# Hybrid decoder block on one core: top-k 2 of the gathered token tile moved into the first steps of the dense expert stage, one-hots and fill products shared out by thirds, 19 + 3 u-tiles ahead

## The chip, the cores and the metric

The kernel runs on one core of a Trainium2 chip. The metric is the device time of one execution in microseconds (us), lower is better. A profile of one execution goes with it: the span of that execution, the busy time of each engine (PE is TensorE's matmuls, PEld its weight loads, DVE is VectorE, ACT is ScalarE, POOL is GpSimd, SP is SyncE, which issues most transfers), the waits, and the order of the instructions in time.

## The reference

512 tokens of width 1024 go through attention and a linear recurrence side by side, then through an expert layer and a gated embedding. The change is in the expert layer, which for each token scores 2 x 128 keys per head, takes the best 16 of each half, then the best 16 of their sums, and mixes the 128 experts so chosen out of 16384:

```
    v1, i1 = lax.top_k(s1, PEER_TOPK)
    v2, i2 = lax.top_k(s2, PEER_TOPK)
    cand = (v1[..., :, None] + v2[..., None, :]).reshape(B, S, PEER_HEADS, PEER_TOPK * PEER_TOPK)
    ...
    top_s, pos = lax.top_k(cand, PEER_TOPK)
    idx = jnp.take_along_axis(cand_idx, pos, axis=-1)
    g = jax.nn.softmax(top_s, axis=-1).astype(x.dtype)
    ...
        act = jax.nn.gelu(jnp.einsum('chkd,cd->chk', ue, xt))
        return jnp.einsum('chk,chkd->cd', gt * act, ve)
```

"Top-k 1" is the choice of 16 keys in each half, "top-k 2" the choice of 16 sums, with the softmax and the expert numbers.

## The kernel before, in words

The 512 tokens are four tiles of 128. **One tile is gathered** (tile 0, NTG = 1): for each of its 128 chosen experts the rows of u and v are fetched by an indirect transfer (line 938, issued by POOL) and used on DVE (lines 946 and 953). **Three tiles are dense**: all 16384 experts are multiplied on PE, and a weight table that is zero but for the chosen experts picks out what counts. There are 128 expert groups e of 128 experts. A *u-tile* of group e is gelu(u_e x), a 128 x 384 tile; it times the weights gives `hf`, which times v_e is added to `y`.

Every operand in fp32 is split into a high and a low part (`split`, lines 54 on ACT and 55 on DVE or POOL) and multiplied three times (`mm3`, lines 64 to 66). Some u-tiles are made as plain fp32 products instead, without a split (`fill`, line 743); these are the *fill products*, 8 for each u-tile, and they are put between other work on PE.

**The weight stage** (some 573 to 785 us of the span) runs 96 groups n, 32 for each dense tile; a third of the stage is one tile. Group n makes the weights of four tokens from a one-hot `bm` (line 863, DVE) and a weighted one-hot `am`. Which engine makes `am` is written in the string PAT: D is DVE (four instructions, line 857), P is POOL (four, line 857), A is ACT (eight, lines 853 and 854). `w_make` multiplies them on PE (line 870), copies the result on ACT to `wst` (line 875), and every eight groups SP writes 2 MB to `wdram`. The steps of top-k 2 are functions in a list, taken from it while n runs: those of tile 2 in the first third (with what is left of top-k 1), those of tile 3 in the second, those of the gathered tile 0 in the last. A third takes its steps in its first 23 groups, and the tile of the next third can start only when they are done. A list has 13 steps: one that builds the candidates, four that find the maxima of two heads each, the start of the softmax, one that splits the positions, four `pick` that look the numbers up, the end of the softmax, and the expert numbers. After group n, `fill` makes fill products up to a due number.

**The dense stage** (from 785 us) runs the groups e = 0 to 127 under a manual schedule: each engine takes its instructions in the order of the program text. Step e loads and splits v_(e+1) (`v_split`, `h_make`), loads and splits u_(e+AHEAD+1), multiplies u-tile e+AHEAD (from e = EXTRA on), fetches gathered rows up to `rate(e)`, uses those fetched one step earlier, and ends with the 18 products of v_e (`v_mm`). Before the loop stand N4 fill tiles and three u-tiles made with splits. The buffers of v and h are double, so PE needs in step e what DVE has made during step e-1. When the u-tiles are done, `pw_load` brings the eight parts of the last gate's matrix, one every second step, and v's low part is made on POOL in every second step. The queue of SP takes its transfers in program order too.

Of the kernel before, what the change touches and what calls it, by code (L numbers as in the profile page):

```python
# [18 lines left out]
NT = S // 128  # L19
KD = D // 128  # L20
EPS = 1e-6
NEG = -1e30
NTG = 1
NTD = NT - NTG
TD = NTD * 128
PAT = "DPADPPADPPADPDAP"
EXTRA = 4
AHEAD = 21
N4, F0 = 22, 5
NCAND = 80  # L30
# [6 lines left out]
def trunk_kernel(ctx: ExitStack, tc: tile.TileContext, x, xT, pT, small, sinkb, rows, w_in, w_ua, w_ul,  # L37
                 w_ab, w_o, w_q, k12, uT, vP, uN, w_pg, w_pp, out):
    nc = tc.nc
# [545 lines left out]
    def u_gelu(e, ps):  # L585
# [5 lines left out]
        acts[e] = a  # L591

    with tc.tile_pool(name="topk", bufs=1, side="right") as T:
        vals = T.tile([128, NT, 16, 16], F32, name="vals")
        idxu = T.tile([128, NT, 16, 16], U32, name="idxu")
        x2f = T.tile([128, KD, TD], F32, name="x2f")
# [3 lines left out]
        def small(name, dt=F32):  # L600
            return T.tile([128, 128], dt, name=name, tag=name, bufs=1)

        def topk2(t, cuts=((0, 8),)):
# [5 lines left out]
            def begin(lo, hi):  # L609
                def run():  # L610
                    if lo == 0:
                        L["idf"] = T.tile([128, 16, 16], BF16, name="idf", tag="idf", bufs=1)
                        L["ii"] = L["idf"].rearrange("p (h z) k -> p h z k", z=2)
                        L["cand"] = T.tile([128, 8, NCAND], F32, name="cand", tag="cand", bufs=1)
                        L["cand2"] = T.tile([128, 8, NCAND], F32, name="cand2", tag="cand2", bufs=1)
                        top[t] = T.tile([128, 8, 16], F32, name="top", tag="top", bufs=1)
                        posu[t] = T.tile([128, 8, 16], U32, name="posu", tag="posu", bufs=1)
                    hs, n = slice(lo, hi), hi - lo
                    nc.vector.tensor_copy(L["idf"][:, 2 * lo:2 * hi], idxu[:, t, 2 * lo:2 * hi])
                    vv = vals[:, t].rearrange("p (h z) k -> p h z k", z=2)  # L620
# [21 lines left out]
            def soft0():  # L642
                g = gg if t < NTG else T.tile([128, 128], F32, name="g", tag="g", bufs=2)
# [26 lines left out]
            def soft1():  # L670
                g = gs[t]
                g3 = g.rearrange("p (h k) -> p h k", h=8)
                sg = T.tile([128, 8], F32, name="sgs", tag="sgs", bufs=2)
                nc.vector.tensor_reduce(sg, g3, AX.X, OP.add)
                nc.vector.reciprocal(sg, sg)
                nc.vector.tensor_tensor(g3, g3, sg[:, :, None].to_broadcast([128, 8, 16]), OP.mult)

            def pick(z, part):
                def run():
                    if part == 0:  # L680
                        L["i", z] = T.tile([128, 128], F32, name=f"i{z}", tag=f"i{z}", bufs=1)
                    hs = slice(4 * part, 4 * part + 4)

                    eq = T.tile([128, 4, 16, 16], BF16, name="eq", tag="eq", bufs=1)
                    ab3 = L["ab"][z].rearrange("p (h k) -> p h k", h=8)[:, hs]
                    nc.vector.tensor_tensor(eq, iota[:, None, None, 0:16].to_broadcast([128, 4, 16, 16]),
                                            ab3[:, :, :, None].to_broadcast([128, 4, 16, 16]), OP.is_equal)
                    nc.vector.tensor_tensor(eq, eq, L["ii"][:, hs, z, None, :].to_broadcast([128, 4, 16, 16]), OP.mult)
                    nc.vector.tensor_reduce(L["i", z].rearrange("p (h k) -> p h k", h=8)[:, hs], eq, AX.X, OP.add)
                return run  # L690

            def end():
                i0, i1 = L["i", 0], L["i", 1]
                if t < NTG:
                    f = T.tile([128, 128], F32, name="fi", tag="fi", bufs=1)
                    nc.vector.scalar_tensor_tensor(f, i0, 128.0, i1, op0=OP.mult, op1=OP.add)
# [57 lines left out]
        with tc.manual_schedule():  # L754
# [33 lines left out]
            def topk1(hh, t):  # L788
                def run():
                    s = scs[hh][:, t * 128:(t + 1) * 128]  # L790
                    v, ix = vals[:, t, hh, :], idxu[:, t, hh, :]
                    w = T.tile([128, 128], F32, name="mr", tag="mr", bufs=3)
# [53 lines left out]
        def a_make(n):  # L846
            t, q = NTG + n // 32, n % 32
            kind = PAT[n % len(PAT)]
            tr, trn = trs[t], trns[t]
# [32 lines left out]
        with tc.manual_schedule():  # L882
            for _ in range(NWR):
                f_load()
            for k, step in enumerate(first):
                fill((F0 * KD * (k + 1)) // len(first))
                step()
            later = [topk2(NTG + 1), topk2(NTG + 2), [s_ for t in range(NTG) for s_ in topk2(t)]]
            later[0] = [f_ for _, f_ in rest] + later[0]
# [4 lines left out]
            def start(n, limit):  # L894
                for m in range(n, min(n + 7, NGRP)):
                    if m // 32 <= limit and m not in begun and m - n <= lead[PAT[m % len(PAT)]]:
                        begun.add(m)
                        a_make(m)
            nb = 0
            for n in range(NGRP):  # L900
# [167 lines left out]
    with tc.manual_schedule():  # L1068
# [17 lines left out]
        for e in range(128):  # L1086
# [96 lines left out]
```

## Time and profile before

| what | us |
|---|---|
| device time, median of 3 runs | 1842.68 (1839.93 to 1848.08) |
| device time of the profiled execution | 1839.95 |
| its span | 1838.2 |
| PE busy in the span | 1735.0 (94%) |
| DVE busy | 1349.1 (73%) |
| ACT busy | 775.7 (42%) |
| POOL busy | 593.0 (32%) |

The spans are counted from the first to the last instruction, so 1.75 us of the execution lie around them. Matmuls overlap each other, so the duration of one is longer than the distance to the next: the time of a row of matmuls is read from the starts, not from the durations. "Idle before" of an instruction is how long its engine stood still ahead of it, and "<-" names what ended that.

### The profile page before, as it was taken

How to read it: one execution, taken by the hardware profiler on the slowest of the kernel's cores; microseconds unless marked ns; L12 is line 12 of the kernel's file. 1: busy time of each engine (PE TensorE's matmuls, PEld its weight loads, DVE VectorE, ACT ScalarE, POOL GpSimd, SP SyncE). 2: the span in 40 equal slices, each digit the busy share in tenths (PEclk: the TensorE clock that was granted, in tenths of full speed). 3: DMA queues.
4: the chain of work that ended last, by engine and by line, in shares of the span. 5: the costliest groups of instructions: out<-in, count | busy, mean ns of one | idle time of the engine just before them, and what ended most of it. 6: DMA issues, size and time to landing. Idle time of an engine off the chain costs nothing.

```text
span 1838.2 us, 23709 instructions
## 1 busy us (share of the span) xinstructions
PE 1735.0 (94%) x8503; PEld 1476.1 (80%) x8503; DVE 1349.1 (73%) x2636; ACT 775.7 (42%) x1253; POOL 593.0 (32%) x465
## 2 busy tenths in 40 slices
PE   6998899999989699989999999999999999999997
PEld 4877777778866477779999999999999998998775
DVE  6545675556998988947877878788887877865766
ACT  3446657333324577733333333333333333333432
POOL 0000000012315689923433434344434443411210
PEclk9999999999999999999999999999999999999999
DMA  5222225452222244388897988989989889863711
GB/s 190 103 92 87 92 88 170 142 187 97 77 69 103 92 184 184 151 305 311 310 350 286 330 321 293 336 291 330 328 284 337 302 299 339 296 257 134 288 48 69
DMA packets 150311, 392.86 MB, mean 214 GB/s; under 512 B 11824, under 2 KB 62256, under 8 KB 148528
## 3 DMA queue, kind: packets, MB, share of 16 engines
q1 hardware_dynamic: 108720, 245.92, 36.9%
q0 software_dynamic: 37440, 136.33, 21.0%
q10 hardware_dynamic: 4032, 9.08, 1.3%
q8 instruction: 67, 1.10, 0.2%
q14 instruction: 52, 0.43, 0.1%
HBM read 355.64 MB, written 35.65 MB: 213 GB/s over the span
## 4 chain that ended last, share of the span: by engine, by line
PE 72%; DVE 19%; ACT 4%; DMA 2%; issue 2%; ACTq 0%; DVEq 0%; SPq 0%
PE y L64 9%; PE y L65 9%; PE y L66 9%; PE u L66 8%; PE u L64 8%; PE u L65 8%; PE bpj L66 3%; PE bpj L64 3%; PE bpj L65 3%; PE u L743 3%; DVE bm L863 2%; PE bg L870 1%; DVE am L857 1%; DVE idxu L797 1%; DVE idxu L794 1%
## 5 line engine op out<-in xcount | busy, mean ns | idle before, releaser
L64 PE MATMUL y<-vh,hxh 128*128 128x512 f32 x768 | 302.1, 393 | 13.0 <-ACT hxh L54 13.0
L65 PE MATMUL y<-vl,hxh 128*128 128x512 f32 x768 | 301.5, 393 | 0.0
L66 PE MATMUL y<-vh,hxl 128*128 128x512 f32 x768 | 301.4, 392 | 0.0
L66 PE MATMUL u<-x2h,wl 128*128 128x384 f32 x848 | 285.2, 336 | 2.0 <-DVE wl L55 2.0
L64 PE MATMUL u<-x2h,wh 128*128 128x384 f32 x848 | 285.2, 336 | 0.8 <-ACT wh L54 0.8
L54 ACT ACTIVATE vh<-vr 128x1024 fp32r<-128x1024 f32 x128 | 135.8, 1061 | 354.8 <-issue 329.0
L65 PE MATMUL u<-x2l,wh 128*128 128x384 f32 x848 | 284.0, 335 | 0.0
L55 DVE TENSOR_TENSOR wl<-wr,wh 128x1024 fp32r<-128x1024 f32 x154 | 188.4, 1225 | 102.6 <-ACT wh L54 101.9
L938 POOL DMA_INDIRECT gb<-in_vP_dram,vg x128 | 175.7, 1373 | 232.2 <-DVE yg L953 204.0
L938 POOL DMA_INDIRECT gb<-in_uN_dram,ug x128 | 166.8, 1303 | 252.5 <-DVE scr L946 228.8
L857 POOL TENSOR_SCALAR am<-iota,tr 128x128 f32<-128x128 f32 x168 | 179.4, 1081 | 70.4 <-ACT tr L706 45.6
L55 POOL TENSOR_TENSOR wl<-wr,wh 128x1024 fp32r<-128x1024 f32 x18 | 43.2, 2404 | 483.0 <-ACT wh L54 477.4
L54 ACT ACTIVATE wh<-wr 128x1024 fp32r<-128x1024 f32 x172 | 180.1, 1048 | 35.8 <-PE bpj L65 21.0
L55 DVE TENSOR_TENSOR vl<-vr,vh 128x1024 fp32r<-128x1024 f32 x118 | 144.4, 1224 | 65.2 <-ACT vh L54 63.1
L54 ACT ACTIVATE hxh<-hf 128x384 fp32r<-128x384 f32 x128 | 67.2, 525 | 267.8 <-DVE hf L975 267.8
L64 PEld LDWEIGHTS y<-vh,hxh 128*128 128x128 f32 x768 | 145.0, 189 | 42.6 <-ACT hxh L54 15.4
L953 DVE SCALAR_TENSOR_TENSOR yg<-gb,cg,yg 128x1024 f32<-128x1024 f32 x127 | 162.9, 1282 | 20.3 <-DMA gb<-in_vP_dram,vg 17.9
L66 PEld LDWEIGHTS y<-vh,hxl 128*128 128x128 f32 x768 | 145.0, 189 | 32.7 <-DVE hxl L55 1.5
L946 DVE SCALAR_TENSOR_TENSOR scr<-gb,x2t 128x1024 f32<-128x1024 f32 x128 | 156.5, 1223 | 16.1 <-DMA gb<-in_uN_dram,ug 13.9
L65 PEld LDWEIGHTS y<-vl,hxh 128*128 128x128 f32 x768 | 145.2, 189 | 26.2
L64 PEld LDWEIGHTS u<-x2h,wh 128*128 128x128 f32 x848 | 159.2, 188 | 5.8 <-ACT wh L54 1.9
L65 PEld LDWEIGHTS u<-x2l,wh 128*128 128x128 f32 x848 | 159.6, 188 | 4.4
(322 smaller groups left out, 3218.4 us busy)
## 6 DMA issues: line engine op xcount, KB each, us to landing
vr<-in_vP_dram SPq DMA_DIRECT2D x128, 512.0 KB, 9.0
wr<-in_uT_dram SPq DMA_DIRECT2D x120, 512.0 KB, 9.1
wt<-wdram SPq DMA_DIRECT2D x32, 768.0 KB, 8.2
wdram<-wst SPq DMA_DIRECT2D x11, 2048.0 KB, 7.2
wr<-in_w_in_dram SPq DMA_DIRECT2D x38, 512.0 KB, 3.3
wr<-in_w_q_dram SPq DMA_DIRECT2D x16, 512.0 KB, 3.3
gdram<-gf ACTq DMA_DIRECT2D x16, 256.0 KB, 2.2
wr<-in_w_ul_dram SPq DMA_DIRECT2D x8, 512.0 KB, 3.3
```

The lines of the kernel that those rows point to most:

```text
L54: nc.scalar.activation(hi, src, AF.Copy)
L55: (lo_eng or nc.gpsimd).tensor_tensor(lo, src, hi.bitcast(F32), OP.subtract)
L64: nc.tensor.matmul(ps, lh, rh, start=first, stop=False)
L65: nc.tensor.matmul(ps, lh, rl, start=False, stop=False)
L66: nc.tensor.matmul(ps, ll, rh, start=False, stop=last)
L743: nc.tensor.matmul(fps[0], raws[e][:, k * 128:(k + 1) * 128], x2f[:, k, :], start=k == 0, stop=k == KD - 1)
L794: nc.vector.max_index(ix[:, 0:8], v[:, 0:8], s)
L857: (nc.vector if kind == "D" else nc.gpsimd).tensor_scalar(am[:, j, :], iota, tr[:, 0, c:c + 1], tr[:, 2, c:c + 1], op0=OP.is_equal, op1=OP ...
L863: nc.vector.tensor_tensor(bm, iota[:, None, :].to_broadcast([128, 4, 128]), trs[t][:, 1, 4 * q:4 * q + 4, None].to_broadcast([128, 4, 128] ...
L938: nc.gpsimd.indirect_dma_start(out=b, out_offset=None, in_=src, in_offset=bass.IndirectOffsetOnAxis(ap=idx[:, k:k + 1], axis=0))
L946: nc.vector.scalar_tensor_tensor(scr, b, 1.0, x2t, op0=OP.mult, op1=OP.mult, accum_out=dots[:, k:k + 1])
L953: nc.vector.scalar_tensor_tensor(yg, b, cg[:, k:k + 1], yg, op0=OP.mult, op1=OP.add)
```

## The change

The dense stage takes over the top-k 2 of the gathered tile: its 13 steps go into steps e = 0 to 4, three a step, behind the splits that the step makes for e+1. For this the tiles that top-k 2 works on move to a pool that stays open (`TK`), and the staging tile of the last gate's matrix has one buffer instead of two. The gathers start later (`rate` is 2.7 a step from e = 5 on; before 1.3 a step from e = 0, then 2.6) and end at the same step, 99 or 100. The tiny copy that held the gathers back until the first weights had landed (`gate`) goes. Three u-tiles fewer are made as fill products (19 instead of 22) and three more in the dense loop, which makes them up to e = 108 instead of 106. The engine of each one-hot is now written down for each third: in the first two thirds one DVE group in 16 becomes an ACT group (4 D, 7 P, 5 A), in the last two POOL groups in 16 become DVE groups (7 D, 5 P, 4 A; before 5 D, 7 P, 4 A). The fill products are 44 in each of the first two thirds and 24 in the last, where there were 1.51 a group throughout.

```
-PAT = "DPADPPADPPADPDAP"
-EXTRA = 4
-AHEAD = 21
-N4, F0 = 22, 5
+PATS = "DPAPDPAPPADPAPDA", "DPAPDPAPPADPAPDA", "DPADPADPDPADPADD"
+EXTRA = 3
+AHEAD = 19
+N4, F0 = 19, 5
...
+    TK = ctx.enter_context(tc.tile_pool(name="lists", bufs=1, side="right"))
...
-            kind = PAT[n % len(PAT)]
+            kind = PATS[n // 32][n % 16]
...
-            later = [topk2(NTG + 1), topk2(NTG + 2), [s_ for t in range(NTG) for s_ in topk2(t)]]
+            later = [topk2(NTG + 1), topk2(NTG + 2), []]
...
-                fill(F0 * KD + (n + 1) * (NF - F0) * KD // (NGRP - 6))
+                m = n + 1
+                fill(F0 * KD + 44 * min(m, 64) // 32 + (24 * max(0, m - 64)) // 26)
...
-        raw = PW.tile([128, 1024], F32, name="wgr", tag="wgr", bufs=2)
+        raw = PW.tile([128, 1024], F32, name="wgr", tag="wgr", bufs=1)
...
-        return min(256, int(2.6 * (e + 1) - 1.4 * max(0, e + AHEAD - 127) - 1.3 * min(EXTRA, e + 1)))
+        return min(256, max(0, int(2.7 * (e - 4))))
...
-
-        gate = E.tile([128, 1], F32, name="gate")
-        nc.gpsimd.tensor_copy(gate, wts[0][:, 0, 0, 0:1])
+        gathered = [s_ for t in range(NTG) for s_ in topk2(t)]
...
+            for step in gathered[3 * e:3 * e + 3]:
+                step()
             for j in range(g0, rate(e)):
                 g_fetch(j)
```

DVE at the border from the second to the last third, before: behind one-hots of the second third come the candidates (`idf`, `cand`) and the first maxima (`top`, `posu`) of the gathered tile's list, mixed with one-hots.

```order
L863 TENSOR_TENSOR bm<-iota,tr 128x512 x3
L619 CAST idf<-idxu 128x256
L622 TENSOR_TENSOR cand<-vals 128x8x16
L624 TENSOR_TENSOR cand<-vals 128x8x56
L627 TENSOR_TENSOR cand<-vals 128x8x8
L857 TENSOR_SCALAR am<-iota,tr 128x128 x4
L863 TENSOR_TENSOR bm<-iota,tr 128x512
L635 MAX top<-cand 128x8
```

The same border in the changed kernel, where the one-hots' lines are 867 and 861: behind the softmax of tile 3 (`sgs`, `g`) there are one-hots alone, up to the end of the stage.

```order
L678 TENSOR_REDUCE sgs<-g 128x8
L679 RECIPROCAL sgs<-sgs 128x8
L680 TENSOR_TENSOR g<-g,sgs 128x128
L867 TENSOR_TENSOR bm<-iota,tr 128x512 x3
L861 TENSOR_SCALAR am<-iota,tr 128x128 x4
L867 TENSOR_TENSOR bm<-iota,tr 128x512 x4
```

The whole list of the gathered tile has left the last third.

DVE in step e = 3 of the dense loop, before: the parts for v_4 and h_4, the low part of u-tile 25, and one use of a gathered row (`scr`).

```order
L55 TENSOR_TENSOR vl<-vr,vh 128x1024
L975 TENSOR_TENSOR hf<-act,wt 128x384
L55 TENSOR_TENSOR hxl<-hf,hxh 128x384
L55 TENSOR_TENSOR wl<-wr,wh 128x1024
L946 SCALAR_TENSOR_TENSOR scr,dots<-gb,x2t 128x1024
```

The same step in the changed kernel:

```order
L55 TENSOR_TENSOR vl<-vr,vh 128x1024
L980 TENSOR_TENSOR hf<-act,wt 128x384
L55 TENSOR_TENSOR hxl<-hf,hxh 128x384
L55 TENSOR_TENSOR wl<-wr,wh 128x1024
L690 TENSOR_TENSOR eq<-iota,aa 128x1024
L692 TENSOR_TENSOR eq<-eq,idf 128x1024
L693 TENSOR_REDUCE i_6830<-eq 128x64
L690 TENSOR_TENSOR eq<-iota,bb 128x1024
L692 TENSOR_TENSOR eq<-eq,idf 128x1024
L693 TENSOR_REDUCE i_6835<-eq 128x64
L678 TENSOR_REDUCE sgs<-gg 128x8
L679 RECIPROCAL sgs<-sgs 128x8
```

Three steps of top-k 2 stand there now ahead of the next step's `vl`, in the place of the use of the gathered row.

ACT in steps e = 1 and 2 of the dense loop of the changed kernel; before, `vh` and `hxh` alternate there with nothing between them.

```order
L54 ACTIVATE hxh<-hf 128x384
L651 ACT_TABLE_LOAD
L651 ACTIVATE gg<-gg 128x128
L54 ACTIVATE vh<-vr 128x1024
L54 ACTIVATE hxh<-hf 128x384
L54 ACTIVATE wh<-wr 128x1024
```

The exponential of the gathered tile's softmax, which needs DVE's four maxima steps, now stands ahead of the high part of v_3.

## Rows read from the trace of the kernel before

**Rows 1.** Busy time of each engine in three stretches, with granted clock and DMA.
```profile
core 0: us, PE busy (x) PEld busy (x) DVE busy (x) ACT busy (x) POOL busy (x), PEclk, DMA share, GB/s
656.00:720.00 64.00, 60.81 (x359) 47.08 (x358) 57.40 (x166) 48.71 (x107) 60.38 (x56) 1.00 0.48 181
...
802.00:850.00 48.00, 46.88 (x216) 40.66 (x217) 34.60 (x48) 17.38 (x24) 14.40 (x10) 0.96 0.85 304
850.00:1000.00 150.00, 150.00 (x761) 136.85 (x760) 118.55 (x167) 52.94 (x74) 61.30 (x48) 1.00 0.88 323
```

**Rows 2.** Chain that ended last, last third: start us, us, what, count.
```profile
720.50 0.66 issue
...
722.41 1.03 DVE am L857 x4
...
767.28 0.65 PE u L743 x2
767.93 0.89 PE bg L870 x8
...
785.29 1.53 DMA wdram<-wst
```

**Rows 3.** Groups of instructions on ACT, 720 to 782 us: busy, mean ns, idle.
```profile
L875 ACT ACTIVATE wst<-bg 128x512 f32<-128x512 f32 x31 | 17.7, 590 | 11.8 <-PE bg L870 11.7
L854 ACT ACTIVATE am<-am,tr,trn 128x128 f32<-128x128 f32 x32 | 15.8, 493 | 1.1
L853 ACT ACTIVATE am<-iota,trn 128x128 f32<-128x128 f32 x32 | 12.4, 388 | 0.0
```

**Rows 4.** DVE in order of time, one maxima step: start us, us, instruction.
```profile
660.27 0.23 DVE L635 MAX8 top<-cand 128x8 f32<-128x80 f32 x1
...
662.91 1.37 DVE L863 TENSOR_TENSOR bm<-iota,tr 128x512 f32<-128x512 f32 x2
```

**Rows 5.** DVE in order of time, positions step and first pick of the gathered tile.
```profile
744.02 0.31 DVE L658 TENSOR_SCALAR q8u<-posu 128x128 uint32<-128x128 uint32 x1
...
746.94 1.22 DVE L686 TENSOR_TENSOR eq<-iota,aa 128x1024 bf16<-128x1024 f32 x1
...
750.05 0.68 DVE L863 TENSOR_TENSOR bm<-iota,tr 128x512 f32<-128x512 f32 x1
```

**Rows 6.** DVE in order of time, start of the dense stage.
```profile
799.76 1.23 DVE L55 TENSOR_TENSOR vl<-vr,vh 128x1024 fp32r<-128x1024 f32 x1 [8.71 <-ACT vh L54]
...
803.37 1.23 DVE L55 TENSOR_TENSOR vl<-vr,vh 128x1024 fp32r<-128x1024 f32 x1 [0.77 <-ACT vh L54]
804.51 0.55 DVE L975 TENSOR_TENSOR hf<-act,wt 128x384 f32<-128x384 f32 x1
805.65 0.56 DVE L55 TENSOR_TENSOR hxl<-hf,hxh 128x384 fp32r<-128x384 f32 x1 [0.59 <-ACT hxh L54]
...
821.04 1.22 DVE L55 TENSOR_TENSOR wl<-wr,wh 128x1024 fp32r<-128x1024 f32 x1 [0.39 <-ACT wh L54]
```

**Rows 7.** PE in order of time, first dense steps: first products of v and u tiles.
```profile
802.06 0.80 PE L64 MATMUL y<-vh,hxh 128*128 128x512 f32 x1 [5.43 <-ACT hxh L54]
...
821.06 0.44 PE L64 MATMUL u<-x2h,wh 128*128 128x384 f32 x1 [0.42 <-ACT wh L54]
...
826.27 0.39 PE L64 MATMUL y<-vh,hxh 128*128 128x512 f32 x1
...
830.38 0.34 PE L64 MATMUL u<-x2h,wh 128*128 128x384 f32 x1
...
838.68 0.34 PE L64 MATMUL u<-x2h,wh 128*128 128x384 f32 x1
```

**Rows 8.** The page's costliest groups: splits of v on ACT, uses of gathered rows.
```profile
L54 ACT ACTIVATE vh<-vr 128x1024 fp32r<-128x1024 f32 x128 | 135.8, 1061 | 354.8 <-issue 329.0
...
L953 DVE SCALAR_TENSOR_TENSOR yg<-gb,cg,yg 128x1024 f32<-128x1024 f32 x127 | 162.9, 1282 | 20.3 <-DMA gb<-in_vP_dram,vg 17.9
```

**Rows 9.** Transfers issued, by tile: count, KB each, median us to landing.
```profile
wgr<-in_w_pg_dram SPq DMA_DIRECT2D x8, 512.0 KB, 6.1
```

More of the change, by code (lines that the diff above doesn't have):

```diff
@@ L591, in u_gelu @@
         acts[e] = a
+    TK = ctx.enter_context(tc.tile_pool(name="lists", bufs=1, side="right"))
     with tc.tile_pool(name="topk", bufs=1, side="right") as T:
-        vals = T.tile([128, NT, 16, 16], F32, name="vals")
-        idxu = T.tile([128, NT, 16, 16], U32, name="idxu")
+        vals, idxu = [], []
+        for t in range(NT):
+            P = TK if t < NTG else T
+            vals.append(P.tile([128, 16, 16], F32, name=f"vals{t}"))
+            idxu.append(P.tile([128, 16, 16], U32, name=f"idxu{t}"))
         x2f = T.tile([128, KD, TD], F32, name="x2f")
@@ L600, in small @@
         def small(name, dt=F32):
-            return T.tile([128, 128], dt, name=name, tag=name, bufs=1)
+            return TK.tile([128, 128], dt, name=name, tag=name, bufs=1)
         def topk2(t, cuts=((0, 8),)):
@@ L611, in run @@
                     if lo == 0:
-                        L["idf"] = T.tile([128, 16, 16], BF16, name="idf", tag="idf", bufs=1)
+                        L["idf"] = TK.tile([128, 16, 16], BF16, name="idf", tag="idf", bufs=1)
                         L["ii"] = L["idf"].rearrange("p (h z) k -> p h z k", z=2)
[L614 to L617, printed above, removed]
+                        L["cand"] = TK.tile([128, 8, NCAND], F32, name="cand", tag="cand", bufs=1)
+                        L["cand2"] = TK.tile([128, 8, NCAND], F32, name="cand2", tag="cand2", bufs=1)
+                        top[t] = TK.tile([128, 8, 16], F32, name="top", tag="top", bufs=1)
+                        posu[t] = TK.tile([128, 8, 16], U32, name="posu", tag="posu", bufs=1)
                     hs, n = slice(lo, hi), hi - lo
-                    nc.vector.tensor_copy(L["idf"][:, 2 * lo:2 * hi], idxu[:, t, 2 * lo:2 * hi])
-                    vv = vals[:, t].rearrange("p (h z) k -> p h z k", z=2)
+                    nc.vector.tensor_copy(L["idf"][:, 2 * lo:2 * hi], idxu[t][:, 2 * lo:2 * hi])
+                    vv = vals[t].rearrange("p (h z) k -> p h z k", z=2)
                     cand = L["cand"]
@@ L642, in soft0 @@
             def soft0():
-                g = gg if t < NTG else T.tile([128, 128], F32, name="g", tag="g", bufs=2)
+                g = gg if t < NTG else TK.tile([128, 128], F32, name="g", tag="g", bufs=2)
                 gs[t] = g
@@ L672, in soft1 @@
                 g3 = g.rearrange("p (h k) -> p h k", h=8)
-                sg = T.tile([128, 8], F32, name="sgs", tag="sgs", bufs=2)
+                sg = TK.tile([128, 8], F32, name="sgs", tag="sgs", bufs=2)
                 nc.vector.tensor_reduce(sg, g3, AX.X, OP.add)
@@ L680, in run @@
                     if part == 0:
-                        L["i", z] = T.tile([128, 128], F32, name=f"i{z}", tag=f"i{z}", bufs=1)
+                        L["i", z] = TK.tile([128, 128], F32, name=f"i{z}", tag=f"i{z}", bufs=1)
                     hs = slice(4 * part, 4 * part + 4)
-                    eq = T.tile([128, 4, 16, 16], BF16, name="eq", tag="eq", bufs=1)
+                    eq = TK.tile([128, 4, 16, 16], BF16, name="eq", tag="eq", bufs=1)
                     ab3 = L["ab"][z].rearrange("p (h k) -> p h k", h=8)[:, hs]
@@ L694, in end @@
                 if t < NTG:
-                    f = T.tile([128, 128], F32, name="fi", tag="fi", bufs=1)
+                    f = TK.tile([128, 128], F32, name="fi", tag="fi", bufs=1)
                     nc.vector.scalar_tensor_tensor(f, i0, 128.0, i1, op0=OP.mult, op1=OP.add)
@@ L790, in run @@
                     s = scs[hh][:, t * 128:(t + 1) * 128]
-                    v, ix = vals[:, t, hh, :], idxu[:, t, hh, :]
+                    v, ix = vals[t][:, hh, :], idxu[t][:, hh, :]
                     w = T.tile([128, 128], F32, name="mr", tag="mr", bufs=3)
@@ L895, in start @@
                 for m in range(n, min(n + 7, NGRP)):
-                    if m // 32 <= limit and m not in begun and m - n <= lead[PAT[m % len(PAT)]]:
+                    if m // 32 <= limit and m not in begun and m - n <= lead[PATS[m // 32][m % 16]]:
                         begun.add(m)
```

## The prediction

> **What bounds the kernel now.** I read the stretches of the span first, then the chain of waits, then the two stretches that the change touches, instruction by instruction. In the dense stage PE sets the time: it is busy 150.00 of 150 us while DVE has 118.55 [rows 1]. A step there takes 8.30 us, from 830.38 to 838.68, of which the 18 products of v take 4.11 (826.27 to 830.38) and a u-tile the other 4.19 [rows 7]. So what is added to PE there is paid in full, and what is added to DVE is hidden while PE has a step in hand. The weight stage is different: in its second third DVE (57.40), POOL (60.38) and PE (60.81) all lie near the 64 us [rows 1]. The chain of the last third starts on DVE at 720.50, goes over to PE before 767.28 and ends with the last `wst` at 785.29, 64.8 us in all [rows 2].
>
> **The weight stage, per part.** A maxima step of top-k 2 takes 662.91 - 660.27 = 2.65 us [rows 4], a pick 750.05 - 746.94 = 3.11, the positions step 746.94 - 744.02 less one `bm` of 0.68 = 2.24 [rows 5]. The other twelve small instructions I put at the 0.22 that one of the ten in the positions step takes: 2.7. The list is 4 x 2.65 + 4 x 3.11 + 2.24 + 2.7 = 28.0 us of DVE, which leave the last third.
>
> What is left there: DVE 32 x 0.68 for `bm` [rows 5] and 14 groups of 1.03 [rows 2], 36 us. PE 32 groups of 0.89 and 24 fill products of 0.65 [rows 2] (767.28 shows one, in two passes), 44 us. ACT 32 copies of 0.59 and eight groups of four pairs of 0.49 + 0.39 [rows 3], 47 us if nothing overlaps. POOL ten groups at 60.38/56 = 1.08 an instruction [rows 1], 43 us. So DVE is out of the way, and what is late next is ACT, with PE and POOL close behind. The third cannot fall below 47; in-order queues waiting for each other I price at 5.5, between nothing and the 11 that would leave it at 58. I take 52.5, **-12.3 us** (-18 to -7).
>
> In each of the first two thirds DVE loses two groups of 1.03; ACT gains two of 3.5, and has room, as it is busy 48.71 of 64 [rows 1]. Some ten groups at a third's end, where PE leads, carry 0.13 fill products fewer, 10 x 0.13 x 0.65 = 0.9. Against more stands POOL: it keeps its 56 instructions, 60.38 of 64 us. I take 2.5 a third, **-5.0** together (0 to -8). The sum for the stage is -17.3.
>
> **Three u-tiles from fill to the dense loop.** Their fill products are in the sum above. On PE, which sets the dense stage, they cost 3 x 4.19 = **+12.6 us**; two stand at e = 107 and 108, one at e = 3.
>
> **The list in the first dense steps.** Here DVE is behind PE. I count from T = 799.76, when DVE starts on v_0, and walk both engines. One step's parts for v and h take 2.76 on DVE (803.37 to 805.65, and 0.48 until the next can start), the low part of a u-tile 0.39 + 1.14 [rows 6]. Without the change PE runs from T + 2.3 and ends step 6 at T + 47.2 (838.68 and one step of 8.30) [rows 7]. With it:
> - e = 0: h_1 done at 6.4 [rows 6], then the candidates and two maxima steps, until 12.6.
> - e = 1: v_2 and h_2 until 15.4, two maxima steps and the softmax's start until 20.9.
> - e = 2: ACT's exponential, which I put at 0.3 by the 0.39 of an instruction of its size [rows 3], stands ahead of the high part of v_3, 1.06 [rows 8]; DVE starts at 22.3, ends v_3, h_3 at 25.0 and the low part of u-tile 22 at 26.6, then positions and two picks until 35.0.
> - e = 3: v_4, h_4 until 37.8, u-tile 23 until 39.3, two picks and the softmax's end until 46.2.
> - e = 4: v_5, h_5 until 49.0, u-tile 24 until 50.5, the expert numbers until 51.4. From e = 5 on DVE has slack again.
>
> PE: v_0 and v_1 end at 12.5 (the first four v tiles of before took 2.2 more than 4 x 4.11, from 802.06 to 821.06 less a wait of 0.42 [rows 7]). v_2 must wait until 15.0. A u-tile that meets its low part as it is made ends 826.27 - 821.04 = 5.2 after DVE starts on that part [rows 6, 7]: u-tile 22 ends at 30.6, v_3 at 34.7; u-tile 23 at 43.4, v_4 at 47.5; u-tile 24 at 54.6, v_5 at 58.7; u-tile 25 and v_6 follow without a wait, until 67.0. That is 19.8 later than before, 4.2 of which is the u-tile at e = 3, already counted. The rest, **+15.6 us**, is a wait of PE for DVE that was not there (14 to 19).
>
> PE's gaps in this walk are 2.5, 6.3, 3.5 and 1.9 us. After its gap of 5.43 at 802.06 the first product took 0.80 where a later one takes 0.39, and the granted clock of that stretch is 0.96, that is partly at 1.2 instead of 2.4 GHz [rows 1, 7]; v_0 lost the 2 us above. I leave the clock out of the sum, since after the larger gaps PE waits for DVE again, which covers a slower tile. The Trainium skill, "TensorE: Matmul & The Clock Gate", section "Why this matters for your kernels", warns against idle gaps between bursts of matmuls, because the clock drops back to half. [...]
>
> **What I cost at nothing.** The gathers start later and end at the same step; their 2.7 uses a step lie beside PE, and the cover is thin (a rival below). `pw_load` with one buffer can ask for its next part only when DVE has finished the last one, two steps earlier. Of two steps of 4.11 its own two splits, 1.06 and 1.23 like those of v [rows 6, 8], leave 5.9 us; the transfer lands in 6.1 at the median [rows 9], now with more transfers queued ahead of it than it will have. So nothing, or at most some 2 us for each of seven. Removing `gate` frees a wait of POOL that nothing hangs on any more.
>
> **Sum.** -17.3 + 12.6 + 15.6 = +10.9. The profiled execution took 1839.95, so 1851; it lies 2.7 below the median of its three runs, 1842.68, and on that scale the forecast is **1854 us**, slower by 0.6%. A measurement of this kernel can tell 0.5% from no change, 9.2 us.
>
> **Rivals.**
> 1. *The thirds give more than I take* (the other side). If the last third falls to ACT's 47 and the first two to POOL's 60.4 and the like, the stage saves 18 + 8 = 26; with the wait at 14 the sum is +1, 1843, no change. For it speaks that all four engines are near balance by count; against it, that POOL is full in two thirds and that ACT's queue holds `wst` behind eight one-hot instructions. It decides from a saving of some 20 us on. It would take 29 to win.
> 2. *The gathers pace DVE.* A step with three uses is 2.76 + 1.53 + 3 x (1.28 + 0.16 of waiting, 20.3/127) [rows 8] = 8.6 us of DVE, one with two 7.2. At 2.7 uses the mean is 8.2, just under PE's 8.30. If the waits for rows double with the denser fetches (the transfer engines are 0.88 busy [rows 1]), it is 8.6, and 0.3 over some 70 steps adds 21: 1875. Against it: the mean rises by 0.1 uses only.
> 3. *The list is hidden after all.* If the first dense steps were held by transfers anyway, the wait goes and -4.7 remains, 1838; with a saving of 22 or more it is faster by over 0.5%. Against it: PE ran v_1 to v_3 before without a gap, and DVE's parts are earlier in its queue than anything that could be late.
> 4. *The weight stage saves only the fill products and two DVE groups a third*, because ACT becomes as slow as DVE was: -5 + 12.6 + 15.6, 1866.
>
> That the change does not do what it says is no rival: the order shows the steps in e = 0 to 4 and none in the last third.
>
> **How the numbers follow.** The forecast's own case has 0.58 (sum +5 to +19), rival 1 0.22, rival 2 0.10, rival 3 0.05, rival 4 0.05. Of the forecast's case about two thirds, 0.39, lie above 9.2 us; with rivals 2 and 4 slower is 0.54. Faster is most of rival 3 and the edge of rival 1, 0.07. The rest, 0.39, is no change. The range takes the forecast with the bounds of its terms, most of rival 1 and rival 4: 1843 to 1868, leaving out rivals 2 and 3 and the edges.
>
> **What would show it.** Right: the last third, from the end of tile 3's softmax to the last `wst`, near 52 us with ACT as the releaser; 872 products of u-tiles on each of the three `mm3` lines; in the first five dense steps PE idle some 14 us, released by ACT's and DVE's splits, with the picks ahead of them on DVE; PE full from e = 6 on. Wrong: PE without gaps in those steps, DVE waiting for gathered rows in steady state with PE idle, or a weight stage more than 20 or less than 10 us shorter.

## The result, and the profile after

The changed kernel takes **1857.35 us** (median of six runs, 1853.38 to 1863.89), the kernel before 1843.1 in runs on the same chip: a ratio of 1.0080, 95% interval 1.0057 to 1.0104. It is slower by 14.3 us; the forecast was 1854 and slower by 0.6%.

The profiled executions have spans of 1859.4 and 1838.2 us, 21.2 apart. Some 7 of that is chance between runs: the profiled one of the changed kernel lies 3.8 above its median, that of the kernel before 3.1 below. The four busy times moved little (PE 1749.3 us and 94%, DVE 1349.5, ACT 788.4, POOL 587.2), so the answer is in the stretches.

Stretches of the changed kernel, in the columns of [rows 1]: inside the second third, the last third (from 16 us after its first copy, as the chain of [rows 2] began), the first seven dense steps, and steady state.

```profile
656.00:720.00 64.00, 59.50 (x356) 46.08 (x355) 55.32 (x159) 55.44 (x126) 62.27 (x57) 1.00 0.43 165
723.30:774.20 50.90, 47.45 (x315) 39.90 (x314) 32.59 (x78) 43.45 (x98) 31.58 (x31) 0.99 0.49 197
789.00:856.00 67.00, 55.24 (x227) 46.19 (x228) 51.53 (x129) 21.28 (x29) 7.03 (x5) 0.87 0.50 177
856.00:1000.00 144.00, 143.76 (x729) 130.41 (x728) 114.11 (x161) 50.04 (x69) 62.94 (x47) 1.00 0.88 318
```

The last third takes 50.9 us where it took 64.8. DVE is out of the way (32.59 us); PE (47.45) and ACT (43.45) are left. In the first dense steps PE is busy for 55.24 of 67 us, and its granted clock is 0.87: that is the new wait. From 856 on PE is full again.

A third begins on ACT with the copy of a tile's numbers, `tr`. First the grouped row of the kernel before (first and last start) and its last weights' copy, then the same row of the changed kernel.

```profile
L706 ACT ACTIVATE tr<-bh x3: 484/491/491, 572.9 to 704.7; 128x384 f32<-128x384 f32 x3
784.67 0.60 ACT L875 ACTIVATE wst<-bg 128x512 f32<-128x512 f32 x1
```

```profile
L710 ACT ACTIVATE tr<-bh x3: 470/485/491, 577.0 to 707.5; 128x384 f32<-128x384 f32 x3
773.55 0.58 ACT L879 ACTIVATE wst<-bg 128x512 f32<-128x512 f32 x1
```

With these marks, the first `vl` of the dense stage (T in the prediction: 799.76 before [rows 6], 787.27 after) and the starts of the u-tiles, the 21 us can be put in their places:

```profile
787.27 1.23 DVE L55 TENSOR_TENSOR vl<-vr,vh 128x1024 fp32r<-128x1024 f32 x1 [6.66 <-DMA vr<-in_vP_dram]
```

| stretch | before | after | difference | forecast |
|---|---|---|---|---|
| up to the first `tr` (code not changed) | 572.9 | 577.0 | +4.1 | 0 |
| first two thirds | 131.8 | 130.5 | -1.3 | -5.0 |
| last third, to the end of the last `wst` | 80.6 | 66.6 | -14.0 | -12.3 |
| from there to T | 14.5 | 13.1 | -1.4 | 0 |
| T to the end of step 6 | 47.2 | 67.9 | +20.7 | +19.8 |
| from there to the last u-tile's start | 822.9 | 841.9 | +19.0 | +16.6 |
| from there to the end | 168.3 | 162.3 | -6.0 | -8.2 |

The forecast's column splits the u-tiles' +12.6 as the prediction did: one in the first dense steps, two at e = 107 and 108, each of those a step of 8.30 in the place of one of v alone. One profile a kernel gives these marks to no better than a few us: the eight kernels that share the change's weight stage up to the last third (the change and seven of those below) put the first `tr` between 570.3 and 580.2 and take 130.5 to 132.8 for the first two thirds. So the +4.1 and the -1.3 lie within chance.

The chain that ended last, end of the last third (start us, us, what, count):

```profile
759.90 0.65 PE u L747 x2
760.54 0.89 PE bg L874 x8
761.44 0.65 PE u L747 x2
762.12 10.44 DMA wr<-in_uT_dram
772.58 1.06 ACT wh L54
773.64 0.49 ACT wst L879
774.15 1.52 DMA wdram<-wst
...
778.15 9.10 DMA vr<-in_vP_dram
```

PE leads up to 761.44, in groups of 0.89 us with a fill product of 0.65 between them. The end hangs on something that the prediction did not name: a late u-tile's raw rows land at 772.58, ACT rounds them, and the last weights' copy stands behind that in ACT's queue.

PE in order of time in the first dense steps of the changed kernel (start us, us, instruction, idle before), the products that begin a tile:

```profile
802.50 0.50 PE L64 MATMUL y<-vh,hxh 128*128 128x512 f32 x1 [2.71 <-ACT hxh L54]
...
813.15 0.69 PE L64 MATMUL u<-x2h,wh 128*128 128x384 f32 x1 [4.52 <-ACT wh L54]
...
819.86 0.40 PE L64 MATMUL y<-vh,hxh 128*128 128x512 f32 x1
...
826.05 0.45 PE L64 MATMUL u<-x2h,wh 128*128 128x384 f32 x1 [1.90 <-ACT wh L54]
...
832.81 0.40 PE L64 MATMUL y<-vh,hxh 128*128 128x512 f32 x1
...
837.58 0.45 PE L64 MATMUL u<-x2h,wh 128*128 128x384 f32 x1 [0.48 <-ACT wh L54]
...
846.91 0.33 PE L64 MATMUL u<-x2h,wh 128*128 128x384 f32 x1
...
855.21 0.33 PE L64 MATMUL u<-x2h,wh 128*128 128x384 f32 x1
```

Where [rows 7] have u-tiles 8.30 apart from the second on, these are 12.90, 11.53, 9.33 and 8.30 apart. DVE in the same steps shows what stands ahead:

```profile
816.39 1.22 DVE L690 TENSOR_TENSOR eq<-iota,aa 128x1024 bf16<-128x1024 f32 x1
...
821.61 1.22 DVE L693 TENSOR_REDUCE i<-eq 128x64 f32<-128x1024 bf16 x1
822.74 1.22 DVE L55 TENSOR_TENSOR vl<-vr,vh 128x1024 fp32r<-128x1024 f32 x1
...
834.28 1.22 DVE L55 TENSOR_TENSOR vl<-vr,vh 128x1024 fp32r<-128x1024 f32 x1
```

Two picks fill the time from 816.39 to the `vl` of 822.74, and two more (with the softmax's end) hold the next `vl` until 834.28. PE's releaser reads "ACT wh", but ACT was itself waiting: `hxh` needs DVE's `hf`, and `wh` stands behind `hxh`. ACT around the exponential:

```profile
802.47 1.28 ACT L651 ACT_TABLE_LOAD   x1
808.55 0.31 ACT L651 ACTIVATE gg<-gg 128x128 f32<-128x128 f32 x1 [4.80 <-DVE gg L650]
808.77 1.04 ACT L54 ACTIVATE vh<-vr 128x1024 fp32r<-128x1024 f32 x1
...
824.52 0.52 ACT L54 ACTIVATE hxh<-hf 128x384 fp32r<-128x384 f32 x1 [10.48 <-DVE hf L980]
```

ACT stands still for 4.80 us with the next row of v in hand, as forecast; the exponential itself is 0.31. The 10.48 us at 824.52 are its wait behind the positions step and the first two picks. The page's row of the u-tiles has the 24 products more on each line of `mm3`:

```profile
L64 PE MATMUL u<-x2h,wh 128*128 128x384 f32 x872 | 293.9, 337 | 9.3 <-ACT wh L54 9.3
```

### The profile page after: what moved, and what is told of

Its sections match the earlier page's. It is cut to its first block, busy times and chain, and to the rows that moved or that the text cites. A ratio compares the mean times of both kernels' runs of the same rounds, so it can differ in the third digit from the quotient of the medians.

```text
span 1859.4 us, 23807 instructions
## 1 busy us (share of the span) xinstructions
PE 1749.3 (94%) x8527; PEld 1487.5 (80%) x8527; DVE 1349.5 (73%) x2640; ACT 788.4 (42%) x1288; POOL 587.2 (32%) x447
## 4 chain that ended last, share of the span: by engine, by line
PE 73%; DVE 18%; ACT 4%; DMA 3%; issue 2%; SPq 0%; ACTq 0%; DVEq 0%
PE y L66 9%; PE y L65 9%; PE y L64 9%; PE u L66 8%; PE u L64 8%; PE u L65 8%; PE bpj L66 3%; PE bpj L64 3%; PE u L747 3%; PE bpj L65 3%; PE bg L874 2%; DVE bm L867 1%; DVE idxu L801 1%; DVE idxu L798 1%; PE bg L64 1%
## 5 line engine op out<-in xcount | busy, mean ns | idle before, releaser
L64 PE MATMUL u<-x2h,wh 128*128 128x384 f32 x872 | 293.9, 337 | 9.3 <-ACT wh L54 9.3
L66 PE MATMUL u<-x2h,wl 128*128 128x384 f32 x872 | 295.2, 339 | 3.9 <-DVE wl L55 3.8
L65 PE MATMUL u<-x2l,wh 128*128 128x384 f32 x872 | 293.4, 336 | 0.0
L943 POOL DMA_INDIRECT gb<-in_uN_dram,ug x128 | 174.6, 1364 | 302.8 <-DVE scr L951 196.6
L943 POOL DMA_INDIRECT gb<-in_vP_dram,vg x128 | 183.3, 1432 | 212.7 <-DVE yg L958 184.3
L861 POOL TENSOR_SCALAR am<-iota,tr 128x128 f32<-128x128 f32 x152 | 160.7, 1069 | 66.8 <-ACT tr L710 46.7
L64 PEld LDWEIGHTS y<-vh,hxh 128*128 128x128 f32 x768 | 145.2, 189 | 44.1 <-ACT hxh L54 16.5
L64 PEld LDWEIGHTS u<-x2h,wh 128*128 128x128 f32 x872 | 165.5, 190 | 15.0 <-ACT wh L54 11.0
L66 PEld LDWEIGHTS u<-x2h,wl 128*128 128x128 f32 x872 | 165.1, 189 | 7.5 <-DVE wl L55 7.3
L65 PEld LDWEIGHTS u<-x2l,wh 128*128 128x128 f32 x872 | 165.3, 190 | 4.9
```

Of the source, the lines that this page charges most:

```text
L64: nc.tensor.matmul(ps, lh, rh, start=first, stop=False)
L65: nc.tensor.matmul(ps, lh, rl, start=False, stop=False)
L66: nc.tensor.matmul(ps, ll, rh, start=False, stop=last)
L861: (nc.vector if kind == "D" else nc.gpsimd).tensor_scalar(am[:, j, :], iota, tr[:, 0, c:c + 1], tr[:, 2, c:c + 1], op0=OP.is_equal, op1=OP ...
L943: nc.gpsimd.indirect_dma_start(out=b, out_offset=None, in_=src, in_offset=bass.IndirectOffsetOnAxis(ap=idx[:, k:k + 1], axis=0))
```

## The experiments

Twelve kernels, each timed beside the kernel before on the same chip. The theory: moving the list shortens the last third and makes the wait of the first dense steps, and the three u-tiles in the loop are a price of their own.

**The list spread over the dense steps.** One step of the list in e = 0 and in each of e = 3 to 12 (two in e = 6 and e = 12), the gathers from e = 13.

```
+SLOT = {0: (0, 1), 3: (1, 2), 4: (2, 3), 5: (3, 4), 6: (4, 6), 7: (6, 7), 8: (7, 8), 9: (8, 9), 10: (9, 10), 11: (10, 11), 12: (11, 13)}
...
-            for step in gathered[3 * e:3 * e + 3]:
+            for step in gathered[SLOT.get(e, (0, 0))[0]:SLOT.get(e, (0, 0))[1]]:
...
-        return min(256, max(0, int(2.7 * (e - 4))))
+        return min(256, max(0, int(2.72 * (e - 12))))
```

> The changed kernel with the 13 steps of the gathered tile's list spread thinly: the candidates in step e = 0, then nothing until u-tiles are made, and one step of the list (two where they are small) in each of e = 3 to 12; the gathers start at e = 13 with 2.72 a step. My theory: the loss is PE's wait for DVE in the first dense steps, because three list steps (8 us) stand ahead of the next step's splits where DVE has only about 4 us to spare. One list step fits, so the wait of 16.5 us goes: 1857 - 16 = 1841 us (1837 to 1846). Rival 'the start is slow by itself' (first transfers of v, PE's clock after its idle time): it stays at 1857 (1854 to 1860). Rival 'gathers pace DVE': the wait goes, but uses squeezed into e = 13 to 107 cost PE time in steady state, 1850 or more.

Measured: 1845.01, ratio 1.0019 (1.0001 to 1.0036). PE's waits from 785 to 852 us (total, times, longest):

```profile
PE y L65 <- ACT hxh L55: 3.6, 1, 3.6
PE u L67 <- DVE wl L56: 0.6, 1, 0.6
PE u L65 <- ACT wh L55: 0.4, 1, 0.4
```

The 3.6 stand ahead of the very first product; after it PE runs through, and step 6 ends 51.1 us after T (836.42 - 785.32), the 47.2 of before and one u-tile. So the wait was the order of the list. Up to the end of step 6 its going is worth 67.9 - 51.1 = 16.8 us; the steps from there to the last u-tile are 4.9 longer than in the change, so that 12 of the 14 come back. The result is 4 above the middle of what was expected: between T and the last u-tile's start this kernel takes 897.9 us, and the kernel with only the three u-tiles (below) 890.5 for the same steps.

**The list back in the last third**, all else as in the change.

```
-            later = [topk2(NTG + 1), topk2(NTG + 2), []]
+            later = [topk2(NTG + 1), topk2(NTG + 2), [s_ for t in range(NTG) for s_ in topk2(t)]]
...
-            for step in gathered[3 * e:3 * e + 3]:
-                step()
```

> The changed kernel with the gathered tile's list back in the last third of the weight stage, all else as changed. My theory: the list is what made the last third long, so from the copy of the last tile's numbers to the last wst it goes from 66.6 back to 78 or more, and the wait of the first dense steps goes: 1857 - 16.5 + 12 = 1853 (1849 to 1857). Rival 'the last third became shorter by the new sharing-out of one-hots and by fewer fill products, not by the list': it stays near 67, and the whole comes to 1841 (1838 to 1845).

Measured: 1857.79, 1.0097 (1.0078 to 1.0117), as the change. Its `tr` row and its last `wst`:

```profile
L710 ACT ACTIVATE tr<-bh x3: 470/484/491, 571.6 to 704.4; 128x384 f32<-128x384 f32 x3
784.95 0.60 ACT L879 ACTIVATE wst<-bg 128x512 f32<-128x512 f32 x1
```

The last third is 81.2 us again, 14.6 more than in the change, and the wait in the first steps is gone. Where the change puts the list, it costs as much as where it was.

**Only the three u-tiles**, in the kernel before. Its gathers stay as they were: `rate` has a 4 where it had EXTRA.

```
-EXTRA = 4
-AHEAD = 21
-N4, F0 = 22, 5
+EXTRA = 3
+AHEAD = 19
+N4, F0 = 19, 5
...
```

> The kernel before with 19 + 3 u-tiles ahead instead of 22 + 3 and nothing else (fill products then 1.24 a group, gathers as before). My theory: the dense stage pays 3 x 4.19 = 12.6 less what two late steps save, about 12; the weight stage gets back only what PE leads, some 25 of 96 groups with 0.27 x 0.65 us less, 4 us: 1843 + 8 = 1851 (1848 to 1855). Rival 'fill products are hidden beside DVE throughout': 1855 or more. Rival 'all of PE's 3 x 5.2 us come back': 1840.

Measured: 1849.45, 1.0044 (1.0026 to 1.0062). Its `tr` row and its last `wst`:

```profile
L706 ACT ACTIVATE tr<-bh x3: 485/490/490, 571.1 to 702.7; 128x384 f32<-128x384 f32 x3
782.31 0.60 ACT L875 ACTIVATE wst<-bg 128x512 f32<-128x512 f32 x1
```

The last third stays at 80.2 us, though PE has 10 fill products (6.5 us) fewer between its marks, of the 24 saved in the whole stage: with the list there, PE does not set it. From T to the last u-tile's start this kernel takes 20.4 us more than the kernel before (890.5 against 870.1), and from there to the end 7.1 less (161.2 against 168.3): the three u-tiles cost 13.3 us in the dense stage.

**One buffer for the last gate's matrix**, in the kernel before.

```
-        raw = PW.tile([128, 1024], F32, name="wgr", tag="wgr", bufs=2)
+        raw = PW.tile([128, 1024], F32, name="wgr", tag="wgr", bufs=1)
```

> The kernel before with one buffer instead of two for the staged parts of the last gate's matrix, and nothing else. My theory: nothing, 1843 (1840 to 1846), and ACT never waits for a part. Rival: each of seven parts lands up to 2 us late on the tight chain of the steps without u-tiles, 1850 to 1857.

Measured: 1842.55, 1.0014 (1.0000 to 1.0027). Next to nothing, as costed.

**The spread with slower gathers**, from the first spread; in SLOT the steps from the second on stand one e sooner.

```
-        return min(256, max(0, int(2.72 * (e - 12))))
+        return min(256, max(0, int(2.6 * (e - 10))))
```

> The change with the list of the gathered tile spread over steps e = 0 to 11 (a step of it in most of them) and the gathers from e = 11 on at 2.60 a step, the slope of the kernel before, where the earlier spread had 2.72 and the change 2.70. Theory: the spread kernel lost some 7 us after its first steps to VectorE waiting for gathered rows (15.9 us of such waits from 1100 to 1300, against some 6 in the kernel before), behind which vl stands; a slope of 2.60 gives most of it back: 1840 us (1837 to 1843). Rival: the lost 7 us were chance of that run, not the slope: 1845, as the earlier spread. Second rival: the gathers now end at e = 109, and what of them runs beside the loads of the last stage makes the end longer: 1847 or more.

Measured: 1846.54, 1.0034 (1.0016 to 1.0052). The theory holds, and so does the longer end of the second rival: from T to the last u-tile's start it takes 890.7 us, 7 less than the first spread, and from there to the end 167.7 instead of 161.1. DVE at the end, where v steps without u-tiles have begun:

```profile
1695.30 4.74 DVE L959 SCALAR_TENSOR_TENSOR yg<-gb,cg,yg 128x1024 f32<-128x1024 f32 x2
```

and PE's waits from 1676 to 1705 us there (0.9 in the first spread):

```profile
PE y L65 <- ACT hxh L55: 4.1, 2, 3.4
```

Two uses that take 1.28 each in [rows 8] take 4.74 while POOL makes v's low part beside them, in a stretch where a step is half as long. So the trace shows POOL's split beside the late uses, not the loads that the rival named.

**The late u-tiles' splits behind the last weights' copy**, in the change.

```
-                if n in (NGRP - 3, NGRP - 1):
-                    u_split(NF + (n == NGRP - 1))
...
             fill(NF * KD)
+            u_split(NF)
+            u_split(NF + 1)
```

> The change with the splits of the first two of the three late u tiles put behind the last copy of the weight stage, instead of ahead of it in groups 93 and 95. Theory: the weight stage of the change ends not on ScalarE's load but on the raw u tile's transfer (landing at 772.58), since the last copy into the weights (773.64) stands behind the u tile's rounding on ScalarE's in-order queue; without it that copy ends some 4 us sooner, and the whole kernel is 3 to 5 us faster than the change: 1853 (1851 to 1855). Rival: the copy is then held by PE or by VectorE's one-hots at the same time, or the u tiles come later by what the stage gains: 1857 (1856 to 1859). On the other side, if the u tiles' products then stand in the first dense steps: 1860.

Measured: 1857.23, 1.0096 (1.0072 to 1.0121): no gain. ACT in order of time:

```profile
766.42 0.60 ACT L879 ACTIVATE wst<-bg 128x512 f32<-128x512 f32 x1 [0.20 <-PE bg L874]
...
781.91 1.06 ACT L54 ACTIVATE vh<-vr 128x1024 fp32r<-128x1024 f32 x1 [1.45 <-DMA vr<-in_vP_dram]
```

The copy ends 62.8 us after the third's `tr` (704.2), 3.8 sooner, as the theory said. But then the first step waits for the row of v, and T is 16.0 us behind the copy instead of 13.1: 2.9 of the 3.8 are given back.

**The old pattern of one-hots in all thirds**, in the change.

```
-PATS = "DPAPDPAPPADPAPDA", "DPAPDPAPPADPAPDA", "DPADPADPDPADPADD"
+PATS = ("DPADPPADPPADPDAP",) * 3
```

> The change with the one-hots of all three thirds shared out by the old pattern (VectorE 5, GpSimd 7, ScalarE 4 of 16). Theory: with the list gone from the last third, TensorE alone sets it (1.54 us a group, 32 groups), and the new shares are worth little there, 0 to 3 us; in the first two thirds they were measured at 2.2 us less and 0.8 more, so about 1 us: 1859 (1857 to 1862). Rival: the new shares were what freed the last third, not the list's going: the last third stays near 80 us by its marks instead of 66.6, and the kernel takes 1866 to 1871.

Measured: 1860.86, 1.0108 (1.0082 to 1.0134). Its `tr` row and last copy:

```profile
L710 ACT ACTIVATE tr<-bh x3: 485/491/491, 573.5 to 705.8; 128x384 f32<-128x384 f32 x3
773.78 0.58 ACT L879 ACTIVATE wst<-bg 128x512 f32<-128x512 f32 x1
```

The first two thirds take 132.3 us and the last 68.6. With the new shares eight kernels take 130.5 to 132.8 for the first two thirds (five of them 132.5 or more), so nothing is shown there; for the last, the change and the two spread kernels without late splits take 66.6 to 67.8, so the new shares are worth 0.8 to 2.0 us. The other 12 or 13 of the 14.0 cannot be put down to the list alone. PE leads the third once the list is gone, and between the marks it makes 37 fill products where it made 55: the 18 more, at 0.65, would be some 12 us of PE (an estimate). The kernel with the list back shows that fewer fill products give nothing while the list stays; a kernel without the list and with all the fill products was not tried.

**Slow spread and late splits together**, the edits of both.

> The slow spread and the late splits together, to look for a kernel faster than both. If both theories hold and add: 1836 (1833 to 1840), below the kernel before by some 6 us. If the late splits give nothing: 1840. If the slow spread gives nothing but the late splits do: 1841. If neither: 1845.

Measured: 1839.89, 0.9993 (0.9974 to 1.0011): no difference from the kernel before. Its end is still 167.3 us long.

**The same, one step sooner and at 2.64 gathers a step**, the list's last three steps in e = 10.

```
-        return min(256, max(0, int(2.6 * (e - 10))))
+        return min(256, max(0, int(2.64 * (e - 9))))
```

> Slow spread and late splits, with the list done one step sooner (its last three steps in e = 10) and the gathers at 2.64 a step from e = 10, so that the last are used by e = 107, ahead of the v-only steps. Theory: the spread at 2.60 won back its 7 us after the first steps, but lost 6.6 us at the end (167.7 us from the last u tile, against 161.1), since two gathers' products on VectorE stood at 4.75 us in step 109 beside GpSimd's split of v; without them the end is 161 to 163 us again: 1835 (1832 to 1839), faster than the kernel before. Rival: 2.64 a step is already too dense, and VectorE's waits for gathered rows cost the 5 us again: 1840 to 1843.

Measured: 1838.17, 0.9975 (0.9963 to 0.9987). The end is 161.8 us; the 2.64 costs PE 0.4 us of waiting.

**And the first row of v ahead of the first block of weights.**

```
-        wt_load(0)
         v_load(0)
+        wt_load(0)
         v_load(1)
```

> The same, with the first row of v (512 KB) issued ahead of the first block of weights (768 KB) on SP's queue. Theory: in the late-split kernels the dense stage begins 16 us after the last weights' copy instead of 13, and its first VectorE operation waits for that row (9.1 us in the transfer); issued first, it lands some 2 us sooner, and so does the first step: 1 to 2 us below the kernel without it, 1834. Rival: the weights, then 2 us later, are what the first step needs next: no difference. On the other side: the row waits for its buffer all the same and holds the weights behind it: 2 to 4 us slower.

Measured: 1834.79, 0.9967 (0.9950 to 0.9984). DVE's first `vl`, in the kernel without this edit and with it:

```profile
788.55 1.23 DVE L56 TENSOR_TENSOR vl<-vr,vh 128x1024 fp32r<-128x1024 f32 x1 [5.88 <-ACT vh L55]
```

```profile
777.81 1.23 DVE L56 TENSOR_TENSOR vl<-vr,vh 128x1024 fp32r<-128x1024 f32 x1 [2.93 <-ACT vh L55]
```

DVE's wait ahead of it is 2.95 shorter; the medians differ by 3.4, with intervals that overlap.

**The kernel before at 2.72 gathers a step.**

```
-        return min(256, int(2.6 * (e + 1) - 1.4 * max(0, e + AHEAD - 127) - 1.3 * min(EXTRA, e + 1)))
+        return min(256, int(2.72 * (e + 1) - 1.4 * max(0, e + AHEAD - 127) - 1.3 * min(EXTRA, e + 1)))
```

> The kernel before with its gathers at 2.72 a step instead of 2.60, nothing else. Theory: near 2.7 a step the gathered rows come too late for VectorE (its waits for them from 900 to 1500 rise from 21 us to some 35), vl stands behind them, and the kernel is 2 to 7 us slower: 1847 (1844 to 1850). Rival: what slowed the spread kernel was its late beginning, not the slope; and gathers that end 4 steps sooner cost nothing: 1842.

Measured: 1854.56, 1.0072 (1.0045 to 1.0098), twice the price that was expected. DVE's waits for gathered rows from 900 to 1500 us, in the kernel before and in this one:

```profile
DVE yg L953 <- DMA gb<-in_vP_dram,vg: 11.6, 9, 3.1
DVE scr L946 <- DMA gb<-in_uN_dram,ug: 9.7, 11, 1.3
```

```profile
DVE yg L953 <- DMA gb<-in_vP_dram,vg: 23.6, 13, 3.5
DVE scr L946 <- DMA gb<-in_uN_dram,ug: 14.9, 13, 2.8
```

From T to the last u-tile's start it takes 882.2 us instead of 870.1.

**The two small edits alone, in the kernel before**: the diffs of the late splits and of the first row of v, as above.

> The kernel before with the two small edits alone: the splits of the late u tiles behind the last weights' copy, and the first row of v ahead of the first block of weights. It tells whether the best kernel so far (1834.8) owes its gain over the kernel before to the moved list or to these two edits. Theory: the edits work alike here: the last copy of the kernel before stands behind one rounding of a u tile (1 us) and the first step waits 11 us for the row of v, so 3 to 4 us are to be had: 1838 (1836 to 1840), and the moved list, spread and with the slower gathers, is worth the remaining 3 us. Rival: the edits give all of it: 1835. Second rival: they give nothing here, since the last third ends on VectorE's list and one-hots: 1842.

Measured: 1836.39, 0.9967 (0.9953 to 0.9982). The rival holds: these two edits give the kernel before all that the best version of the change has over it. DVE's first `vl`:

```profile
798.16 1.23 DVE L55 TENSOR_TENSOR vl<-vr,vh 128x1024 fp32r<-128x1024 f32 x1 [2.93 <-ACT vh L54]
```

The wait of 8.71 ahead of the first `vl` in [rows 6] is 2.93 here, and T lies 92.4 us behind the last `tr` instead of 95.1. Which of the two edits gives how much was not tried.

## Why the prediction was right, and where not

**The wait in the first dense steps** was the term that decided, and it held: +15.6 forecast, 20.7 - 4.2 = 16.5 measured. The walk of two queues met DVE's own times to within a microsecond: `vl` for v_3 at T + 22.3 in the walk and T + 22.6 in the trace (809.84), the picks' ends at 35.0 and 46.2 against 35.5 and 47.0, the end of step 6 at 67.0 against 67.9. The spread kernel shows that this wait is the order of the list, as it goes when the same 13 steps stand one, or two short ones, to a step.

**The clock.** After the gaps of 4.52 and 1.90 us the u-tiles take 6.71 (813.15 to 819.86) and 6.76 us (826.05 to 832.81) instead of 4.16 (846.91 to 851.07). The granted clock in these two is 0.66 and 0.75, that is in part the lower level of 1.2 GHz, and 0.87 over the stretch. The Trainium skill, "TensorE: Matmul & The Clock Gate", section "Why this matters for your kernels", warns that idle gaps between bursts of matmuls bring the clock back to half. The trace agrees for the gap of 4.52, and shows a slow u-tile behind the 1.90 too. Leaving the clock out of the sum was right for the reason given: from 800 to 843 us neither DVE nor ACT waits for PE, so a slower tile only shortens PE's next gap, and gaps that the walk has at 6.3, 3.5 and 1.9 us are 4.52, 1.90 and 0.48. The u-tile after the last one has a granted clock of 1.00 and ends 5.19 after its start, as one at full clock does that meets its low part (5.2 in the prediction).

**The weight stage**: -17.3 forecast, -16.7 measured with the way to T. The sum was right by luck, by two errors that met. The last third's -12.3 was -14.0, and the step that failed is the releaser: "what is late next is ACT" was PE first (groups of 1.54 us) and then a transfer. ACT's 47 us by count were 43.45. PE's 44 stand in the trace (256 `bg` and 48 passes of fill in the 50.9 us). With two counts 3 us apart I let the larger decide, and I left out the late u-tiles at the end of the stage, whose raw rows come by SP's queue. The first two thirds' -5.0 was -1.3: the step "DVE loses two groups of 1.03, ACT has room" does not hold. Over the profiles no gain is left of it (130.5 to 132.8 us with the new shares, 131.6 to 132.3 in the six kernels with the old). That POOL, busy for 62.27 of 64 us, sets these thirds fits this, but no run shows it.

**The u-tiles**: +12.6 forecast; +4.2 in the first steps, +16.6 for two steps, -6.0 at the end, 14.8 together. The end gave 6.0 back instead of 8.2, and the traces say where: from the last u-tile's start to the end of the last v product it is 98.1 us instead of 106.4, 8.3 less as forecast, and the part behind that is 64.2 instead of 61.9. Of these 2.3, some 1.5 lie in a stretch of the last gate's products where the granted clock is 0.90 (1820 to 1837; 1.00 from 1801 to 1816 in the kernel before). The rest goes with the one buffer: the part behind the last v product is 61.9 in all four kernels with two buffers, the one with only the three u-tiles among them, and 62.6 or more in every kernel with one; why is open.

**What was costed at nothing**: the buffer was right to within a us (1.0014, 1.0000 to 1.0027, by itself). The gathers were not quite: "the cover is thin" is how it was put, and steady state is 2.4 us longer (2.0 to 3.0 in the four kernels with the change's gathers), with DVE's waits for gathered rows at 34.4 us from 900 to 1500 instead of 21.3. PE's own waits there went only from 0.6 to 1.5. Rival 2 named a mechanism that exists, and not the price: the kernel before at 2.72 loses 12 us to it, but at the change's 2.70 its 21 us did not come.

So -16.7 + 14.8 + 16.5 + 2.4 = +17.0 between the profiles, and +4.1 ahead of the stage in code that the change leaves alone. That makes the 21 us between the two spans, of which the medians keep 14.3. The forecast of +10.9 is 3.4 below the medians and 6.1 below the 17.0; of the 6.1, 4.6 are the gathers and the end. That it came so near the medians is in part chance between runs.

**The rivals.** Rival 1 (the thirds give so much that nothing is lost) asked for 20 us or more from the stage; it gave 16.7. Rival 3 (the list is hidden) is out by PE's gaps, rival 4 by the last third. What none of them said: with the list spread, the gathers at 2.64 and ahead of the v-only steps, and two edits at the border of the stages, the moved list is as fast as the list left in place with those same two edits (0.9967 both). Between these two the last third is 17.1 us shorter with the list moved (61.6 against 78.7), and the dense loop up to the last u-tile's start 22.9 longer (891.0 against 868.1), of which the end gives back 5.1 (164.2 against 169.3). Of these 17.8 us, 13.3 are the price of the three u-tiles by the kernel with only them: most of what the moved list frees, they take. And they belong to it, if the estimate above holds, since with their fill products still in the last third PE would keep it long. Whether 22 fill tiles could stay beside the list's tiles was not tried.

## What to carry to other kernels

When work leaves a stage that one engine sets, look at the transfers and at the in-order queues at the stage's border as well as at the engines' sums: here the next bound was PE, then a raw tile's rounding ahead of the last copy, and behind that a row of v behind the weights in one queue. Work that moved into a stage where another engine sets the time was free here only one piece at a time: three list steps a step cost 16.5 us, one (or two short ones) a step nothing. And when a move makes something denser (2.6 to 2.7 gathers a step), price that by itself, in a run, before it is called covered.

## What the hardware showed that was not expected

**The gathers' knee.** At 2.60 and 2.64 a step PE waits 0 to 1.7 us in steady state, at 2.70 1.5; at 2.72 it waits 4.4 in the spread kernel and 9.0 in the kernel before, and the steps up to the last u-tile are some 7 and 12 longer. DVE's waits for gathered rows do not show where it begins: at 2.64 they are already 30.8 and 31.4 us. The transfer engines' share from 900 to 1500 us tells nothing of it: 0.87 in the kernel before, 0.88 in that kernel at 2.72, 0.89 in the change. Why the two at 2.72 differ is open.

**DVE beside POOL.** The two `yg` that took 4.74 us stood beside a split of v on POOL of 2.48 that began 0.15 us ahead of them; two take 2.6 by [rows 8]. The kernel before has such meetings too:

```profile
1697.17 2.44 POOL L55 TENSOR_TENSOR vl<-vr,vh 128x1024 fp32r<-128x1024 f32 x1 [6.83 <-ACT vh L54]
1698.00 2.02 DVE L55 TENSOR_TENSOR hxl<-hf,hxh 128x384 fp32r<-128x384 f32 x1 [0.65 <-ACT hxh L54]
```

This `hxl` takes 2.02 us instead of 0.56, and ends 0.41 behind POOL's split.

**The table load.** The exponential brings an ACT_TABLE_LOAD of 1.28 us, which the prediction had left out, but it is issued ahead of the wait for DVE and ends 4.8 us before the exponential can start, so it cost nothing. The Trainium skill, "ScalarE: Activation LUTs", section "What ACT_TABLE_LOAD costs", gives the load about the same time (some 1283 ns) and a drain of about 1380 ns with it. The load agrees; a drain of that length does not show: this load begins 0.02 us behind the instruction ahead of it, and behind the load back to the u-tiles' function (826.01, 1.28 us) the activation starts at 827.30.
